# Moving the drains of VectorE and GpSimd into a hold of a matmul kernel, and giving ScalarE drains too

## The chip, the cores and the metric

The kernel runs on one core of one Trainium2 chip. The metric is the device time of the whole program in microseconds (us), as the median of several executions. A second kernel is called faster or slower when it differs by over 2%.

A *drain* is an instruction that waits until its engine has finished what it was given. Here drains are used only as filler: an engine that passes a few more instructions reaches sooner the point at which its next block of instructions is fetched from memory.

## The reference

```python
x_flat = x.reshape(-1, in_dim)            # 32768 x 256, float32
y = x_flat @ W                            # W: 256 x 256
lora_out = x_flat @ lora_A                # rank 16
lora_out = lora_out * lora_E
lora_out = lora_out @ lora_B
y = y + scale * lora_out
```

So 33.5 MB of x are read and 33.5 MB of y are written. The kernel folds the low-rank part into W once and then does one matrix product.

## The kernel before

x is cut into four chunks of 64 rows in each of 128 partitions, which live in three buffers ("homes"), so chunk 3 takes the place of chunk 0. SyncE issues all large loads (L) and stores (S) in this order:

```python
ORDER = [("A",),
    ("L", 0, 0, 16), ("L", 0, 16, 40), ("L", 0, 40, 64),
    ("L", 1, 0, 32), ("L", 1, 32, 64),
    ("L", 2, 0, 64),
    ("S", 0, 0, 40), ("S", 0, 40, 64),
    ("L", 3, 0, 32), ("L", 3, 32, 64),
    ("S", 1, 0, 64), ("S", 2, 2, 62), ("S", 3, 0, 64)]
SHARED, END_ROWS = 2, 2
SHARES = (slice(108, 113), slice(0, 108), slice(113, P))   # by GpSimd: chunk 2's first and last 2 rows
HELD = (2, 0)                       # chunk 2's first group waits ...
HOLDERS = (("S", 0, 0, 40),)        # ... for chunk 0's first store to land
VECTOR_DRAINS = 9
GPSIMD_DRAINS = 7
```

The hold divides the work of the compute engines into two bursts, one until about 54 us and one from 76 to 124 us. The rows are worked in 64 groups of four. GpSimd casts a group to bf16, TensorE transposes it, VectorE copies the transposed group out of PSUM, TensorE multiplies it, and ScalarE copies the result home.

```python
# GpSimd, after it has made the identity
for _ in range(GPSIMD_DRAINS):
    gpsimd.drain()
for g in range(N_GROUPS):
    ...                                        # waits for the group's load
    if (c, b) == HELD:
        for op in HOLDERS:
            gpsimd.wait_ge(stored[op], 16)     # the hold
    ...
    gpsimd.tensor_copy(out=stage[g % NS][:], in_=home(c)[:, b:b + CG, :])...
# VectorE, for g == 0, behind the folded weights
    for _ in range(VECTOR_DRAINS):
        vector.drain()
# TensorE
for i in range(UNROLL):                        # inside a hardware loop
    turn(i + 1, i)
    multiply(i)
```

## Time and profile before

| | before |
|---|---|
| median of 3 runs | 161.36 us (161.2 to 161.93) |
| data moved | 67.43 MB, 422 GB/s in the mean |
| TensorE busy | 94.8 us, 59% of the span |
| GpSimd, ScalarE, VectorE busy | 69.1, 66.1, 45.4 us |

The view of the costliest groups of the kernel before shows why no compute engine is the bound. Columns: line, engine, operation, tiles and shapes, count, busy us, mean ns of one, idle us before it and what ended the most of that.

```profile
L193 POOL CAST stage<-home 128x1024 bf16<-128x1024 f32 x64 | 66.3, 1042 | 50.3 <-DMA out_dram<-home 23.4
L212 ACT COPY home<-psum_y 128x1024 f32<-128x1024 f32 x64 | 64.8, 1012 | 56.1 <-PE psum_y L260 56.1
```

The busiest two helpers each idle for over 50 us. GpSimd's longest wait, 23.4 us, is for a store to land: that is the hold.

### The profile page before, as it was taken

How to read it: one execution, taken by the hardware profiler on the slowest of the kernel's cores; microseconds unless marked ns; L12 is line 12 of the kernel's file. 1: busy time of each engine (PE TensorE's matmuls, PEld its weight loads, DVE VectorE, ACT ScalarE, POOL GpSimd, SP SyncE). 2: the span in 40 equal slices, each digit the busy share in tenths (PEclk: the TensorE clock that was granted, in tenths of full speed). 3: DMA queues.
4: the chain of work that ended last, by engine and by line, in shares of the span. 5: the costliest groups of instructions: out<-in, count | busy, mean ns of one | idle time of the engine just before them, and what ended most of it. 6: DMA issues, size and time to landing. Idle time of an engine off the chain costs nothing.

```text
span 160.0 us, 2041 instructions
## 1 busy us (share of the span) xinstructions
PE 94.8 (59%) x782; PEld 83.4 (52%) x782; DVE 45.4 (28%) x66; ACT 66.1 (41%) x65; POOL 69.1 (43%) x73
## 2 busy tenths in 40 slices
PE   2769999979999600000799999999997000000000
PEld 1248999969999500000689999999996000000000
DVE  0133555545555300000135555555552000000000
ACT  3003777757777700000047777777777000000000
POOL 1074877487777000000647777777775000000000
PEclk9986999999999985555569999999999855555555
DMA  7999999999969997989999999999989996989976
GB/s 270 427 461 424 436 416 467 451 393 418 615 279 524 477 311 318 430 389 432 424 483 401 418 475 418 516 395 393 524 355 399 481 504 291 526 381 459 506 308 262
DMA packets 2451, 67.43 MB, mean 422 GB/s; under 512 B 512, under 2 KB 528, under 8 KB 784
## 3 DMA queue, kind: packets, MB, share of 16 engines
q1 hardware_dynamic: 2016, 66.60, 97.4%
q0 software_dynamic: 224, 0.52, 0.9%
q10 hardware_dynamic: 208, 0.28, 0.7%
q14 instruction: 3, 0.02, 0.0%
HBM read 33.85 MB, written 33.55 MB: 421 GB/s over the span
## 4 chain that ended last, share of the span: by engine, by line
PE 39%; DMA 35%; POOL 1%; ACT 1%; DVE 0%; issue 0%; SPq 0%; ACTq 0%; POOLq 0%; DVEq 0%
DMA out_dram<-home 30%; PE psum_y L260 25%; PE psum_xt L249 13%; DMA home<-in_x_dram 5%; POOL stage L193 1%; ACT home L212 1%; PE psum_y L282 1%; DVE weff L235 0%; SPq L146 0%; ACTq L216 0%; POOLq L192 0%; DVEq L234 0%
## 5 line engine op out<-in xcount | busy, mean ns | idle before, releaser
L193 POOL CAST stage<-home 128x1024 bf16<-128x1024 f32 x64 | 66.3, 1042 | 50.3 <-DMA out_dram<-home 23.4
L212 ACT COPY home<-psum_y 128x1024 f32<-128x1024 f32 x64 | 64.8, 1012 | 56.1 <-PE psum_y L260 56.1
L260 PE MATMUL psum_y<-weff,xt 128*128 128x256 bf16 x512 | 69.0, 280 | 0.0
L231 DVE COPY xt<-psum_xt 128x1024 bf16<-128x1024 bf16 x64 | 44.3, 692 | 68.6 <-PE psum_xt L249 68.6
L249 PE MATMUL psum_xt<-ident,stage 128*128 128x128 f32 x260 | 41.3, 283 | 25.5 <-POOL stage L193 25.3
L260 PEld LDWEIGHTS psum_y<-weff,xt 128*128 128x128 bf16 x512 | 51.5, 101 | 6.1
L249 PEld LDWEIGHTS psum_xt<-ident,stage 128*128 128x128 f32 x260 | 31.8, 146 | 28.0 <-issue 26.6
L273 PE MATMUL psum_y<-ident 128*128 128x512 f32 x4 | 3.8, 1101 | 2.9 <-POOL ident L172 2.9
L273 PEld LDWEIGHTS psum_y<-ident 128*128 128x128 f32 x4 | 1.2, 326 | 3.9 <-POOL ident L172 2.9
L221 DVE TENSOR_SCALAR ate<-psum_y,e_sb 16x256 f32<-16x256 f32 x1 | 0.5, 472 | 7.2 <-PE psum_y L276 7.2
L167 POOL DMA_DIRECT2D out_dram<-home x3 | 2.0, 676 | 1.0 <-PE psum_xt L249 1.0
L212 ACT ACT_TABLE_LOAD x1 | 1.3, 1283 | 2.1 <-SPq L295 2.1
L282 PE MATMUL psum_y<-b_sb,ate 16*128 16x256 f32 x4 | 1.1, 400 | 0.0
L170 POOL MEMSET ident<- 128x128 f32 x1 | 0.2, 205 | 1.7 <-SPq L295 1.7
L276 PEld LDWEIGHTS psum_y<-ident,a_sb 128*16 128x16 f32 x2 | 0.3, 138 | 1.2 <-issue 1.2
L235 DVE TENSOR_TENSOR weff<-w_sb,psum_y 128x512 bf16<-128x512 f32 x1 | 0.7, 686 | 0.4 <-PE psum_y L282 0.4
L282 PEld LDWEIGHTS psum_y<-b_sb,ate 16*128 16x128 f32 x4 | 0.7, 184 | 0.2 <-issue 0.2
L276 PE MATMUL psum_y<-ident,a_sb 128*16 128x128 f32 x2 | 0.6, 421 | 0.0
L172 POOL TENSOR_SCALAR_AFFINE_SELECT ident<-ident 128x128 f32<-128x128 f32 x1 | 0.3, 284 | 0.2 <-POOL ident L170 0.2
L317 POOL MEMSET const-float32-0.0<- 128x1 f32 x1 | 0.1, 93 | 0.2 <-issue 0.2
L317 POOL MEMSET const-bfloat16-1.0<- 128x1 bf16 x1 | 0.1, 97 | 0.0
L317 POOL MEMSET const-uint8-127<- 128x1 uint8 x1 | 0.1, 97 | 0.0
(1 smaller groups left out, 0.1 us busy)
## 6 DMA issues: line engine op xcount, KB each, us to landing
home<-in_x_dram SPq DMA_DIRECT2D x4, 4096.0 KB, 24.6
out_dram<-home SPq DMA_DIRECT2D x1, 7680.0 KB, 37.0
home<-in_x_dram SPq DMA_DIRECT2D x2, 3072.0 KB, 16.7
out_dram<-home SPq DMA_DIRECT2D x1, 5120.0 KB, 48.4
out_dram<-home SPq DMA_DIRECT2D x1, 3072.0 KB, 46.7
home<-in_x_dram SPq DMA_DIRECT2D x1, 2048.0 KB, 7.6
out_dram<-home POOLq DMA_DIRECT2D x1, 432.0 KB, 31.1
w_sb<-in_W_dram ACTq DMA_DIRECT2D x1, 256.0 KB, 2.7
```

The source lines that it names most:

```text
L167: engine.dma_start(out=ends_of(y_chunks[SHARED]), in_=ends_of(home(SHARED))).then_inc(landed, 16)
L193: gpsimd.tensor_copy(out=stage[g % NS][:], in_=home(c)[:, b:b + CG, :]).then_inc(s_stage[g % UNROLL], 1)
L212: scalar.copy(out=home(c)[:, b:b + CG, :], in_=psum_y[g % NY][:]).then_inc(s_free[(g + NY) % UNROLL], 1)
L221: vector.tensor_scalar(out=ate[:], in0=psum_y[0][:R, :KT, :P], scalar1=e_sb[:], scalar2=float(scale), op0=ALU.mult, op1=ALU.mult,).then_in ...
L231: vector.tensor_copy(out=xt[g % NX][:], in_=psum_xt[g % NT][:].bitcast(BF16)).then_inc(s_xt[g % UNROLL], 1)
L235: vector.tensor_add(out=weff[:], in0=w_sb[:], in1=psum_y[1][:, :KT, :]).then_inc(s_free[0], 1)
L249: ins = tensor.transpose(psum_xt[i % NT][:, b, :], words[:, b, :], ident[:])
L260: ins = tensor.matmul(psum_y[i % NY][:, b, :], xt[i % NX][:, b, t::KT], weff[:, t, :], start=(t == 0), stop=(t == KT - 1),)
L273: tensor.matmul(psum_y[1][:, :2, :], ident[:], ident[:, None, :].to_broadcast([P, 4, P]), start=True, stop=True)
L276: ins = tensor.transpose(psum_y[0][:R, t, :P], a_sb[:, t, :], ident[:])
L282: ins = tensor.matmul(psum_y[1][:, t, :], ate[:, t, :], b_sb[:], start=True, stop=True)
L317: nc = _bacc.Bacc("TRN2", target_bir_lowering=False, num_devices=1)
```

## The change

The intent: the three blocks of instructions that VectorE, ScalarE and GpSimd fetch during the run should be fetched inside the hold, once chunk 2 has landed, and at no other time. The early drains go; 12, 10 and 22 drains stand in front of group 32 instead, behind a wait for chunk 2's load.

```diff
-VECTOR_DRAINS = 9
-GPSIMD_DRAINS = 7
+VECTOR_DRAINS = 12
+GPSIMD_DRAINS = 10
+SCALAR_DRAINS = 22
...
+    def drain(engine, n):
+        for op, landed in loaded.items():
+            if op[1:3] == HELD:
+                engine.wait_ge(landed, 16)
+        for _ in range(n):
+            engine.drain()
...  gpsimd_program
-        for _ in range(GPSIMD_DRAINS):
-            gpsimd.drain()
...
             if (c, b) == HELD:
+                drain(gpsimd, GPSIMD_DRAINS)
                 for op in HOLDERS:
...  scalar_program
             c, b = g // GPC, g % GPC * CG
+            if (c, b) == HELD:
+                drain(scalar, SCALAR_DRAINS)
             scalar.wait_ge(s_y, g + 1)
...  vector_program
         for g in range(N_GROUPS):
+            if (g // GPC, g % GPC * CG) == HELD:
+                drain(vector, VECTOR_DRAINS)
             vector.wait_ge(s_turned, g + 1)
...
-                for _ in range(VECTOR_DRAINS):
-                    vector.drain()
```

## The prediction

> **What bounds the kernel now.** I read the page's slices first, then the DMA queues, then the windows by stage.
>
> ```profile
> DMA  7999999999969997989999999999989996989976
> GB/s 270 427 461 424 436 416 467 451 393 418 615 279 524 477 311 318 430 389 432 424 483 401 418 475 418 516 395 393 524 355 399 481 504 291 526 381 459 506 308 262
> q1 hardware_dynamic: 2016, 66.60, 97.4%
> q14 instruction: 3, 0.02, 0.0%
> HBM read 33.85 MB, written 33.55 MB: 421 GB/s over the span
> ```
>
> The DMA row stays at 9 from the second slice to the last few (a lone 6 or 7 is a large packet counted in the slice in which it starts). The queue of the big loads and stores takes 97.4% of what 16 DMA engines have in the span. So this is a copy of 67 MB with arithmetic under it; the time changes only if a DMA engine has less to do, or waits less. The queue named instruction is the one that the change is about: three packets, nearly nothing.
>
> Then the stages (columns: stretch, its length, busy time of PE, PEld, DVE, ACT, POOL, granted clock, DMA share, GB/s):
>
> ```profile
> 8.00:58.00 50.00, 44.34 (x380) 39.69 (x380) 22.83 (x33) 31.37 (x31) 33.06 (x32) 0.97 1.00 433
> 58.00:62.00 4.00, 0.00 (x0) 0.00 (x0) 0.00 (x0) 0.00 (x0) 0.00 (x0) 0.61 1.14 354
> 62.00:75.00 13.00, 0.00 (x0) 0.00 (x0) 0.00 (x0) 0.00 (x0) 0.00 (x0) 0.50 0.97 420
> 125.00:154.00 29.00, 0.00 (x0) 0.00 (x0) 0.00 (x0) 0.00 (x0) 0.00 (x0) 0.54 0.97 419
> 154.00:160.00 6.00, 0.00 (x0) 0.00 (x0) 0.00 (x0) 0.00 (x0) 0.00 (x0) 0.50 0.70 300
> ```
>
> No compute engine works in 58 to 75 us (the hold) or after 125 us, while the DMA share is 0.97 to 1.14: the hold costs the transfers nothing. The longest pieces of the chain and the waits name what ends the hold:
>
> ```profile
> 27.18 48.41 DMA out_dram<-home
> 75.70 1.05 POOL stage L193
> ...
> POOL stage L193 <- DMA out_dram<-home: 23.4, 1, 23.4
> ```
>
> The first store of chunk 0 is issued at 27.18 and lands at 75.59, and GpSimd, 23.4 us idle, starts at 75.70. The last store is issued at 124.28, and the store before it, still moving then, lands at 140.4. So the compute has 16 us of slack before the DMA engines would run dry.
>
> Last, I cut the DMA view into stretches to place the three fetches. The stretches 55 to 56, 80 to 81 and 107 to 108 us answer in turn, and all others from 0 to 160 us show no such row:
>
> ```profile
> q14 instruction: 1, 0.01, 2.1%
> ...
> q14 instruction: 1, 0.01, 1.9%
> ...
> q14 instruction: 1, 0.01, 1.9%
> ```
>
> From here on I use the trace's packet records, which I strung into 16 back-to-back chains, one for each DMA engine, by matching each packet's start to another's end. The names of the chains (A, B, C) are mine. Fetches start at 55.72 (chain A, 333 ns), 80.22 (chain B, 309 ns) and 107.74 us (chain C, 309 ns). No chain is idle for over 0.1 us from 6 us on.
>
> **What the Trainium skill says.**
> - "Runtime: NRT & Kernel Launch", section "Instruction fetch mechanics": an engine's instructions are streamed into a small buffer, and its sequencer drives a DMA queue of its own that fetches the next block while the present one runs; blocks of 16 KiB. The trace agrees on a separate queue; its packets have 8192 bytes, half the page's block.
> - "DMA: Bandwidth & Descriptors", section "Queues, rings and completion order": a DMA engine takes turns between its queues, a packet at a time. The trace agrees: the first fetch starts at 55.719, where a 65536-byte packet of chain A ends (55.722).
> - The same page, "Why a DMA increments its semaphore by 16 and not by 1": engines finish independently, and only all 16 mean that the data is there. The trace agrees: chunk 2's load has 15 landings by 62.62 and the last at 63.49; the hold's store has 15 by 74.72 and the last at 75.59.
> - "Perfetto Trace Analysis", section "Per-engine timelines" (sequencer-only instruction): of a drain the profile reports the execution alone, not its wait. The trace has drains of 10 ns, 40 ns apart, on VectorE, and of 34 ns, 61 ns apart, on GpSimd.
>
> **The change part by part.**
>
> *Removed at the start.* VectorE's 9 drains run from 11.83 to 12.18 us, and its next copy starts at 12.28 on TensorE's transposes, which end at 12.24. GpSimd's 7 end at 3.26, and its first cast waits for data until 8.05. Neither was on the path: 0 us.
>
> *Added in the hold.* VectorE 12 x 40 ns = 0.5 us; GpSimd 10 x 61 ns = 0.6 us; ScalarE 22, about 1 us if 40 to 50 ns apart (an estimate from the other two engines). They start when chunk 2 has landed (63.49 now, near 62.6 if no engine is late) and so end near 64, about 10 us before the store lands. These engines are idle until 75.7 anyway: 0 us.
>
> *Do the fetches move?* A fetch seems to follow the count of instructions an engine has issued. At 107.74 ScalarE has issued 64; the packet ahead on chain C began at 105.33, when it had issued 62. With the change it has 40 + 22 = 62 behind it in the hold and a copy queued: just enough, so the third fetch should be ScalarE's. VectorE has 49 issued in the hold now and 52 after; GpSimd has 57 and a wait, and some 60 after; the fetch at 80.22 comes when they have 50 and 61. So the two early fetches are theirs in some order, and all three should fall at 63 to 66 us (start of the drains, plus at most the 1.5 us packet under way on each chain). I give 0.8 to all three moving.
>
> *What a fetch costs its DMA engine.* Chain C: 0.31 us plus 0.16 us by which the next packet is longer than the median of its size: 0.47 us. Chain B: 0.31 + 0.09 = 0.40 us. Chain A is worse: at the end of chunk 2's load it is at 63.15, the other fifteen at 61.6 to 62.3, mean about 61.9: 1.25 us behind. At the end of chunk 3's load it is at 102.45 against about 100.7: 1.8 us behind. A chain that arrives late at a turn from loads to stores seems to lose again there. Moved behind the landing, A's fetch should cost 0.45 us and the first such loss should go: A gains 0.8 us by 75 us and 0.8 to 1.3 us in all.
>
> *What that is worth at the end.* The shares of chunk 2 that GpSimd stores are cut so that late chains carry less: A and C get 8 KB, most others 41 KB, some 1.2 us more. The last packets end, in order from the back, at 159.60 (A), 159.49, 159.39, 159.32 (B), 159.24 and so on down to 158.50 (C). If A falls to about 158.5, the next chain, which never carried a fetch, still ends at 159.49. So the sum is 159.60 - 159.49 = 0.11 us off the end. B and C only exchange one time of fetch for another. The hold should end at about 74.9, being the last other chain's 74.7 plus what a fetched chain lags, 0.7 us earlier, but this only starts compute with slack sooner. 161.36 - 0.1, rounded with a little hope for the other turns: 161.2 us.
>
> **The rivals.**
> *1. The fetch on A feeds the slow spot.* In 58 to 62 us, just after the first fetch, all sixteen chains have one packet that takes 3.5 to 3.8 us in place of 2.42 (354 GB/s in the window above). If the late chain or its fetch causes that, 1.2 us go for all: 160.1 us. For it: the time. Against it: the other two fetches are followed by nothing like it, and the packets begin to be slow 2.4 us after the fetch. I give it 0.12.
> *2. Three chains late where one was.* The fetches now all come ahead of the hold's store landing and the turns at 82 and 100 us; if each late chain loses 0.5 us or more at each turn, and B, which carries a full share, becomes last: 159.32 + 0.5 to 1 gives 0.2 to 0.7 us more, so 161.6 to 162.1 us. Against it: B was 0.4 us late at 100 us already and lost only 0.08 us there. 0.15.
> *3. A fetch starves an engine.* The steady period of 1.31 us in the second burst goes on over the fetch at 107.74, so nothing is starved now, and nothing will be. A stall of a few us would also be swallowed by the slack of 16 us. 0 us either way.
> *4. Drains are too few*, and a fetch comes when compute resumes at 75 us: the same cost on the same chain, and the same end. 161.2 to 161.4 us.
>
> **Range and chances.** The main path gives 161.2; the three runs of before spread by 0.7 us on their own. Rival 1 reaches 160.1, rival 2 162.1, each with a small chance. I take 160.6 to 161.7. Two per cent would be 3.2 us, more than all fetches and the slow spot together: faster 0.01, within 2% 0.98, slower 0.01.
>
> **What would show it.** All three instruction packets between 62 and 67 us and none later; chunk 2's load with all 16 landings within 0.7 us; the hold's end near 74.9; chain A no longer the last, and the last packet at 159.4 to 159.6; 67.4 MB as before. Wrong would be: the slow spot at 58 to 62 us gone (rival 1), the chains of the fetches last by over 0.3 us (rival 2), or fetches still at 75 to 110 us (rival 4, and the count of drains misjudged).

## The result, and the profile after

| | before | after |
|---|---|---|
| median of 6 runs each | 161.65 us (161.03 to 162.02) | 161.35 us (161.2 to 161.38) |
| ratio | | 0.9983, 95% interval 0.9958 to 1.0008 |
| drains in the hold | none | 12 VectorE at 62.73 to 63.19 us, 10 GpSimd at 62.79 to 63.38 us |
| instruction fetches | 55.72, 80.22, 107.74 us | 67.83, 67.84, 84.82 us |
| chunk 2's load: 15th and 16th landing | 62.62, 63.49 us | 62.57, 62.70 us |
| hold's store: 15th and 16th landing | 74.72, 75.59 us | 75.02, 75.04 us |
| last landing of all | 159.94 us | 159.99 us |

A ratio is the mean time of one kernel's fast runs over that of the other's of the same rounds, so it is not quite the ratio of the medians.

The slices and the instruction queue of the page after:

```profile
DMA  7999999999969997999999999989979997989986
q14 instruction: 3, 0.02, 0.0%
```

The DMA row is as full as before, and there are still three fetches. The DMA view in the stretches 67 to 69 and 84 to 86 us of the changed kernel places them:

```profile
q14 instruction: 2, 0.02, 1.9%
...
q14 instruction: 1, 0.01, 1.0%
```

Two came into the hold, a few us later than intended; the third did not. The chain and the waits of the changed kernel show the hold's end:

```profile
29.86 45.17 DMA out_dram<-home
75.09 1.05 POOL stage L200
...
POOL stage L200 <- DMA out_dram<-home: 21.2, 1, 21.2
```

It ends at 75.09 us, 0.6 us earlier than before (75.70). (The store is issued later, at 29.86 us, because TensorE ran slowly for longer at the start of this execution: a multiplication took 421 ns in place of 272 until about 17 us, not 14. The changed kernel's second trace, after_again, has 27.18 us again. It does not reach the end of the hold.) Last, the stages, with columns as in the prediction:

```profile
58.00:62.00 4.00, 0.00 (x0) 0.00 (x0) 0.00 (x0) 0.00 (x0) 0.00 (x0) 0.67 1.15 365
62.00:75.00 13.00, 0.00 (x0) 0.00 (x0) 0.00 (x0) 0.00 (x0) 0.00 (x0) 0.50 0.97 418
125.00:154.00 29.00, 0.00 (x0) 0.00 (x0) 0.00 (x0) 0.00 (x0) 0.00 (x0) 0.50 0.97 415
```

The rates are within about 3% of those before, the slow stretch at 58 to 62 us included (365 GB/s against 354).

So 0.6 us were won at the hold and none at the end, as the DMA engines were full either way. Where did ScalarE's drains go? The timeline of the changed kernel (start, us, engine, line and operation, idle before it and its releaser):

```profile
79.11 1.01 ACT L221 COPY home<-psum_y 128x1024 f32<-128x1024 f32 x1 [21.80 <-PE psum_y L269]
...
81.45 1.93 ACT L221 COPY home<-psum_y 128x1024 f32<-128x1024 f32 x2 [1.33 <-PE psum_y L269]
...
82.52 0.14 PEld L258 LDWEIGHTS psum_xt<-ident,stage 128*128 128x128 f32 x1 [0.29 <-ACT home L221]
```

The copy at 79.11 is that of group 31. TensorE turns group 32 before it multiplies group 31, and group 32 is what the hold holds; so group 31's copy waits for the hold's end too (21.80 us), and ScalarE's drains, which stand behind it, run at 80.2 to 81.4 us, after the hold. There they delay the next copy to 81.45 and cost TensorE a wait of 0.29 us, which the slack of the compute takes up.

### The profile page after: what moved, and what is told of

Its sections match the earlier page's. It is cut to its first block, busy times and chain, and to the rows that moved or that the text cites. A ratio compares the mean times of both kernels' runs of the same rounds, so it can differ in the third digit from the quotient of the medians.

```text
span 160.0 us, 2070 instructions
## 1 busy us (share of the span) xinstructions
PE 96.5 (60%) x782; PEld 84.4 (53%) x782; DVE 45.4 (28%) x66; ACT 66.0 (41%) x65; POOL 69.3 (43%) x73
## 4 chain that ended last, share of the span: by engine, by line
PE 38%; DMA 33%; ACT 3%; POOL 1%; issue 1%; ACTq 0%; SPq 0%
DMA out_dram<-home 28%; PE psum_y L269 24%; PE psum_xt L258 13%; DMA home<-in_x_dram 5%; ACT home L221 3%; POOL stage L200 1%; PE psum_y L291 1%; SPq L147 0%; ACTq L175 0%; ACTq L225 0%
## 5 line engine op out<-in xcount | busy, mean ns | idle before, releaser
L258 PE MATMUL psum_xt<-ident,stage 128*128 128x128 f32 x260 | 42.2, 286 | 22.3 <-POOL stage L200 22.3
L258 PEld LDWEIGHTS psum_xt<-ident,stage 128*128 128x128 f32 x260 | 32.4, 148 | 25.2 <-issue 23.6
L291 PE MATMUL psum_y<-b_sb,ate 16*128 16x256 f32 x4 | 2.1, 670 | 0.0
L291 PEld LDWEIGHTS psum_y<-b_sb,ate 16*128 16x128 f32 x4 | 1.2, 320 | 0.5 <-issue 0.3
```

The source lines that it names most:

```text
L258: ins = tensor.transpose(psum_xt[i % NT][:, b, :], words[:, b, :], ident[:])
L291: ins = tensor.matmul(psum_y[1][:, t, :], ate[:, t, :], b_sb[:], start=True, stop=True)
```

## The experiments

Three jobs of four kernels, five rounds each, every job on another chip. A kernel under test has 6 runs; the old kernel ran 11 times beside each job. "Chains" are the DMA engines as strung together from the packet records. For these experiments I rebuilt them with one more condition, that an engine moves exactly 8 packets of each large transfer: the one-line matching of the prediction had confused some of them.

### The changed kernel again (after_again, after_third), and the old one as a candidate (before_again)

No edit in any of the three.

> The changed kernel unaltered, for its spread. Theory T1 (a fetch ahead of the turn from chunk 2's load to the first store makes one DMA engine late by 1.2 us or more, and how late depends on where it falls, so the old kernel's times spread): this one stays within 161.2 to 161.5 us, while the runs of the kernel before beside it spread over 161.0 to 162.0. Rival T2 (the spread of before is chance of the chip that day): both spread by about the same. Its trace: two fetches at 66 to 70 us, the third, ScalarE's, behind the hold at about 85 us.

Measured: 161.24 us (161.03 to 161.48), ratio 0.9977; the old kernel beside it 161.56 (161.07 to 162.06). Fetches at 68.08, 68.09 and 84.98 us.

> The kernel before, unaltered, for its spread and one more trace. Theory T1: over 1 us from the fastest to the slowest run, and if the traced execution is one of 161.8 us or more, its trace has a DMA engine that is later at the turns than in the trace at hand (over 1.2 us behind the others at chunk 2's landing, or a last packet over 160.0 us). Rival: a slow execution shows no late engine, and all sixteen are later by the same.

Measured: 161.25 us (161.16 to 161.44), ratio 0.9986 *to itself*: the old kernel beside it had 161.61 (161.08 to 161.92). Its traced execution was not slow, so no slow one was seen in a trace.

> The changed kernel a third time, in another place of the order: 161.2 to 161.4 us if its level is its own; 161.0 us if the lead of the kernel without drains was the order's. Level with the old kernel when that ran as one of the four (161.25 us).

Measured: 161.10 us (160.96 to 161.36), ratio 0.9985. Between the two expectations, 0.1 us from each.

What follows: the spread of the old kernel's runs, which I had put down to its first fetch, is absent when the same code runs in the place of a candidate. T1 fails there. The 0.3 us between the medians of the first result need no effect of the change: the old program compared with itself gives 0.9986 (interval 0.9967 to 1.0005), the changed one 0.9983, 0.9977 and 0.9985, all inside that interval. In like places, though in different jobs, the old kernel has 161.25 us and the changed one 161.35, 161.24 and 161.10. The change moves the time by nothing that can be told from zero. Why the old kernel's runs beside a job spread by 1 us is left open.

The second trace of the old kernel also tests what the prediction rests on. Its first fetch is at 56.04 us, but chunk 2's load has its last two landings only 0.35 us apart (0.87 in the first trace). The engine with that fetch ends at 158.89 us, 0.67 us ahead of the last one, which carries no fetch and ends at 159.56. So chain A's large lag and its last place belong to one execution of the old kernel and not to the kernel.

### No drains at all (none, none_again)

```diff
-VECTOR_DRAINS = 12
-GPSIMD_DRAINS = 10
-SCALAR_DRAINS = 22
+VECTOR_DRAINS = 0
+GPSIMD_DRAINS = 0
+SCALAR_DRAINS = 0
```

> No drains anywhere. By the counts of issued instructions at which the fetches were asked for so far (VectorE about 43, ScalarE about 55, GpSimd about 59 of the traced ones), all three fetches fall in the second burst: VectorE's and GpSimd's at 83 to 95 us, ScalarE's near 107 us. T1: nothing is fetched ahead of the turn at 58 to 62 us, so no engine is late there, and the time is that of the changed kernel, 161.2 to 161.5 us, with a small spread: the drains of before did the harm, and those of after only undo it. Rival T3 (the hold is a better place for a fetch than a burst): slower than the changed kernel by 0.3 us or more, 161.7 us.

Measured: 161.00 us (160.87 to 161.02), ratio 0.9963. The fetches came at 79.27, 88.44 and 105.19 us, all behind the hold. T1 had forecast 161.2 to 161.5 us, so it misses here too.

> The kernel without drains once more, now behind another program and beside the changed kernel. If the 0.2 us by which it led the kernels with drains belongs to it: 160.9 to 161.1 us again, and 0.15 us or more under the changed kernel of the same job. If it was the chip's or the order's: within 0.1 us of that one.

Measured: 161.02 us (160.90 to 161.30), ratio 0.9981; beside it the changed kernel (after_third) had 161.10. So the lead is 0.24 us in the first job and 0.08 us in the third: the level fits the first expectation, the lead the second, and whether there is a lead stays undecided. The wait for the hold's store in the first of these (none):

```profile
POOL stage L200 <- DMA out_dram<-home: 22.2, 1, 22.2
```

The hold there ends at 74.64 us, earlier than in any kernel with a fetch between chunk 2's last packets and the store's landing (75.09 to 75.99 us). The store's 15th and 16th landings are at 74.33 and 74.43 us. The next run, which has drains but no fetch so early, agrees with 74.45 us. The hold was not a better place for the fetches (T3 falls).

### The drains behind all work (drains_at_end)

```diff
-            if (c, b) == HELD:
-                drain(scalar, SCALAR_DRAINS)
...
+        drain(scalar, SCALAR_DRAINS)      # and likewise for the two others, behind their last work
```

> All 44 drains are in the program, but behind each engine's last work, where they bring no fetch forward; the code has the changed kernel's length. If the gain of the run without drains (161.0 us) comes from where its fetches fall, this is 160.9 to 161.1 us as well, with fetches at about 79, 88 and 105 us. If that gain was chance, or the code's length, it is 161.2 to 161.4 us like the changed kernel.

Measured: 161.02 us (160.96 to 161.34), ratio 0.9977, fetches at 89.35, 100.28 and 105.04 us: all behind the hold, though two later than expected. The code is as long as the changed kernel's and the time is that of the kernel without drains. So if there is a lead, it does not go with the length of the code. No changed kernel ran in this job: beside it the old one as a candidate had 161.25 us.

### ScalarE's drains really in the hold (act_in_hold)

```diff
-            if (c, b) == HELD:
+            if ((g + 1) // GPC, (g + 1) % GPC * CG) == HELD:
                 drain(scalar, SCALAR_DRAINS)
```

> ScalarE's 22 drains one group earlier, ahead of the copy of group 31, which itself waits for the hold's end; so they run at chunk 2's landing, near 63 us, and its fetch comes at 66 to 70 us with the two others in place of about 85 us. T1: a fetch is a fetch once it is behind the turn, so 161.2 to 161.5 us as the changed kernel. T3: 0.2 us faster than the changed kernel, 161.1 us.

Measured: 161.18 us (161.10 to 161.46), ratio 0.9976. The DMA view from 67 to 69 us, then the timeline:

```profile
q14 instruction: 3, 0.02, 2.9%
...
81.77 1.01 ACT L221 COPY home<-psum_y 128x1024 f32<-128x1024 f32 x1 [1.20 <-PE psum_y L269]
```

One group earlier, ScalarE's drains start at 62.71 us and its fetch joins the two others, at 68.03, 68.11 and 68.11 us. This shows that group 31's copy was what kept them out of the hold. The second line is the next copy: it now starts when TensorE's product is done (81.73 us), with no drains in between. The time is that of the changed kernel, so the miss cost nothing.

### Drains at the start of the hold (no_landing_wait)

```diff
     def drain(engine, n):
-        for op, landed in loaded.items():
-            if op[1:3] == HELD:
-                engine.wait_ge(landed, 16)
         for _ in range(n):
...  (GpSimd's drains moved ahead of its wait for the load)
```

> VectorE's and GpSimd's drains as in the changed kernel, but without the wait for chunk 2's landing: they run at the start of the hold, 53 to 56 us, and with some three packets of 2.4 us ahead of each fetch these come at about 60 to 63 us, at the turn from load to store. T1: two engines are late by 1 us or more at the end of chunk 2's load, the hold ends at 75.4 us or later, and the time is 0.3 to 0.7 us over that of the changed kernel: 161.6 to 162.0 us. Rival T2 (places of fetches do not matter): 161.2 to 161.5 us.

Measured: 161.17 us (161.14 to 161.22), ratio 0.9976. Only one fetch moved to the turn, at 62.08 us; the others came at 80.22 and 86.18. By the count of issued instructions the one at 80.22 should be GpSimd's, whose drains stop at 61 issued: one or a few too few. The engine hit is late, though not quite as expected: its last packet of the load ends on time, at 62.09 us, and the fetch comes between it and the word of its landing. Chunk 2's load has 15 landings by 62.64 and the last at 63.44, and the waits read

```profile
POOL stage L198 <- DMA out_dram<-home: 22.9, 1, 22.9
```

with the hold's end at 75.42 us. But the time is not 0.3 us over the changed kernel, it is level. An engine that is late at the turn costs the hold 0.8 us (74.64 without drains, in the same job) and the end nothing that can be seen.

### One more fetch for two engines (double_fetch)

```diff
-VECTOR_DRAINS = 12
-GPSIMD_DRAINS = 10
+VECTOR_DRAINS = 144
+GPSIMD_DRAINS = 142
```

> The changed kernel with 132 more drains on each of VectorE and GpSimd behind chunk 2's landing, so that each fetches one more block[...] within the hold: the cost of a fetch by itself. VectorE 144 x 40 ns = 5.8 us and GpSimd 142 x 61 ns = 8.7 us still end by 72 us. If a fetch costs its DMA engine 0.66 to 0.69 us, as the two at 67.8 us of the changed kernel did, and nothing takes it off again: two engines 0.6 us later at the hold's store, the hold's end at 75.6 us or later, and the time 0.4 to 0.7 us over the changed kernel, 161.7 to 162.0 us, since the last of those two ends level with the last of the others already. If the fetches are hidden: 161.2 to 161.4 us.

Measured: 161.76 us (161.70 to 161.90), ratio 1.0022; beside it the changed kernel had 161.10. The page and, below it, the DMA view from 72 to 77 us:

```profile
q14 instruction: 5, 0.04, 0.1%
...
q14 instruction: 2, 0.02, 0.8%
```

Two fetches more, at 73.15 and 76.16 us, the second behind the hold's end (75.99). The kernel is 0.66 us slower than the changed one beside it, clear of the noise. The hold's store has its last landing at 75.94 us. It is that of the engine with the fetches at 67.96 and 73.15 us: the two cost it 1.46 us within the store, each being 0.31 to 0.32 us and a next packet 0.36 and 0.48 us longer.

But the 0.66 us are not shown to be the price of these fetches. In the trace that engine ends at 159.71 us, and the one that ends last, at 160.07, carries no fetch. Its packets of the hold's store take up to 1.68 us in place of 1.51, 0.55 us in all, from 63.4 to 73.0 us, just while the added drains run (62.6 to 71.8 us); in the changed kernel they all take 1.51. So the 264 drains may cost something by themselves, and no run separates the two. What a single fetch costs is seen on its engine alone, and the time did not show it in any other run. Where had those fetches their slack?

### Equal shares (none_equal_shares)

```diff
-SHARES = (slice(108, 113), slice(0, 108), slice(113, P))
+SHARES = (slice(0, P),)
```

> Without drains, and GpSimd's shares of chunk 2 as one transfer of 128 partitions, 8 for each DMA engine, in place of 10 or 11 for twelve engines and 2 for four. If the four lightened engines are those that carry the three fetches and the one with longer packets in chunk 1's store, these now end last: 6 more packets of 159 ns or so, about 1.0 us, against a loss on the others of 0.3 us: 161.6 to 162.0 us. If the shares did not matter, 161.0 us.

Measured: 161.75 us (161.72 to 162.05), ratio 1.0018: 0.75 us over the kernel without drains. In the traces of before and after, the chain with the fetch at 55.72 us, those at 80.22 and 107.74, and a fourth without a fetch have 2 packets of GpSimd's shares, the twelve others 8 to 12. With equal shares each has 8. Then that fourth chain ends last, at 160.22 us, the three with fetches end at 159.14 to 159.34, and the rest earlier. So the uneven shares take the fetches in: each light chain is spared about 8 packets of 159 ns, 1.3 us, an estimate from those packets. But the 0.75 us are the fourth chain's, whose 64 KB packets take about 0.15 us more each in chunk 1's store. The three with fetches end only 0.14 to 0.34 us behind the last of the others (159.00), so without the fourth equal shares would have cost about that (an estimate from these ends). The fourth is also the engine that ends last in double_fetch.

### Chunk 2's load in halves (none_split_l2), and the first store between them (none_store_early)

```diff
-    ("L", 2, 0, 64),
-    ("S", 0, 0, 40),
+    ("L", 2, 0, 32),
+    ("L", 2, 32, 64),      # none_split_l2: the store follows here
+    ("S", 0, 0, 40),       # none_store_early: the store between the halves
```

> Without drains, and chunk 2's load in two halves, so that its packets have 32 KB in place of 64 KB. All 16 engines have one packet about 1.2 us too long at the end of this load, in every trace so far, and none at the end of chunk 3's load, whose packets have 32 KB. If the size of the last packet makes it, the loss goes and the time is 160.0 us, faster than all so far. If the turn from pure load to pure store with no compute running makes it, or something at 58 us of the clock, it stays: 161.0 us, with the long packets again at 58 to 62 us.

Measured: 161.08 us (160.97 to 161.29), ratio 0.9974. The loss stays and is now spread over the last two packets of 32 KB of each engine, 0.7 and 0.5 us.

> Without drains; chunk 2's load in two halves with the first store of chunk 0 between them. All traces so far have all 16 engines slow at 58 to 62 us, the end of chunk 2's load, 1.0 to 1.3 us each in the mean, and hardly any loss at the end of chunk 3's load, when the compute engines run. If the loss belongs to a turn from load to store that no compute accompanies, the turn now at 52 us, in the first burst, is free, the later ones may lose, and the time is 160.0 to 160.8 us. If it belongs to this store following a load, the loss comes at 49 to 52 us; if to 58 to 62 us of the clock, it stays there; in both 161.0 us.

Measured: 161.42 us (161.13 to 163.30), ratio 1.0026: no gain. But the loss moved. The view by stages of none and of none_store_early, 57 to 63 us:

```profile
57.00:63.00 6.00, 0.00 (x0) 0.00 (x0) 0.00 (x0) 0.00 (x0) 0.00 (x0) 0.63 0.83 284
```

```profile
57.00:63.00 6.00, 0.00 (x0) 0.00 (x0) 0.00 (x0) 0.00 (x0) 0.00 (x0) 0.76 1.01 437
```

The stretch runs at full rate, and by the packet records the sixteen engines lose 0.95 us each in the mean at 48 to 52 us instead, where the first half of the load now ends, while all compute engines are busy. So the loss has nothing to do with the fetches, the hold or the clock time: it goes with the program's first large store following a load. What makes it is open. At the end of chunk 3's load, which stores follow too, it is nearly absent.

## Why the prediction was right or wrong

The time was right: 161.2 us forecast, 161.35 measured, within 160.6 to 161.7. Its class, "same", was right. Neither says much for the steps, since the old kernel's 161.65 and 161.25 us lie in that range as well. By its steps:

- **The bound.** Right. The DMA rows of before and after are alike, and five kernels with the fetches at other places between 62 and 108 us (none, none_again, drains_at_end, act_in_hold, no_landing_wait) lie at 161.00 to 161.18 us.
- **Removed drains and added drains cost nothing.** Right for VectorE and GpSimd (0.5 and 0.6 us at 62.7 to 63.4). ScalarE's cost TensorE 0.29 us behind the hold, inside the slack.
- **"All three should fall at 63 to 66 us".** Wrong in two ways. The step that failed for ScalarE was "40 + 22 = 62 behind it in the hold and a copy queued": the copy of group 31 comes ahead of the drains and waits for the hold's end, so the fetch came at 84.82 us; act_in_hold shows it. For the two others "at most the 1.5 us packet under way" was wrong: they came at 67.8, some 4.5 us behind the last drains, about three packets of 1.51 us. At 84.82 us, with packets of 1.21 us, the delay behind the start of the last drain (81.27) was 3.55 us, again about three.
- **What a fetch costs.** Mis-sized where it falls among the hold's stores: 0.66 to 0.70 us there, in place of 0.45. The extra loss of a late engine at the turn was there in this trace (landings 0.87 us apart before, 0.13 after), and the hold's end came at 75.09, with 74.9 forecast. But it was taken from one execution: in before_again the landings are 0.35 us apart. The reading of the slow spot was also short, as chain A's own packet there took 4.03 us, above the 3.5 to 3.8 given for all.
- **The end: "159.60 - 159.49 = 0.11 us off".** Not seen: the last chain ended at 159.67 and carried a fetch again. The step that failed was "If A falls to about 158.5". The fetches moved, but two chains now pay 0.7 us each. That alone does not put them last: at 138.9 us, after the light shares, both are level with the others (138.4 to 139.1). They fall behind in the last store, where five 64 KB packets of each take 2.45 to 2.61 us in place of 2.42 and one packet of GpSimd's shares takes 0.67 and 0.81 us in place of 0.16. Why is open. And the start of the sum, chain A as the last one, does not hold in before_again. Also "B, which carries a full share" was an error of my chain matching: all three chains with fetches are light.
- **Rivals.** 1 fell: 365 GB/s in the slow stretch with the fetch gone from before it, 354 with it, and the stretch follows the store, not the fetch. 2 fell in its time: three chains fetching at 68 us (act_in_hold) gave 161.18 us. 3 held: no gap of a few us. 4 happened for ScalarE, by another cause, and cost nothing, as it said.
- **Never in the prediction:** that the old kernel compared with itself gives 0.9986. What looked like a small gain is of that size.

The lowest times are those of the kernel with no drains, 161.00 and 161.02 us. Its lead over the changed kernel is 0.08 to 0.24 us, about 0.1%, and not settled; that it would come from the fetches lying behind the hold is argued and not shown.

## What to carry to other kernels

Where the transfers are the bound, moving a small cost between places helps only if it comes off the DMA engine that ends last; look at the engines' single ends and shares before moving it, and in more than one trace, since another engine can be the last in the next execution. Before an instruction is put "in a hold", ask of each engine separately what it is waiting on there: an engine a stage further down may still have the previous group ahead of it. And for effects of a few parts in a thousand, run the old kernel as a candidate too.

## What the Trainium skill lacked or had wrong

- "Runtime: NRT & Kernel Launch", section "Instruction fetch mechanics", gives blocks of 16 KiB (256 instructions); every fetch in these traces has 8192 bytes, and 132 more instructions of 64 bytes on an engine brought one more (double_fetch).
- The same section calls the cost "mostly hidden". For the engines that run the instructions nothing here contradicts it: none has a gap of a few us at a fetch. It does not tell what a fetch costs a DMA engine that is full: 0.31 us for the packet and mostly 0.1 to 0.5 us on the next one.
- "DMA: Bandwidth & Descriptors", section "Queues, rings and completion order", has an engine take turns between its queues packet by packet. The fetches do start at a packet's end, but about three packets behind the last of the drains that brought them on (4.5 us with packets of 1.51 us, 3.55 us with 1.21 us); no page tells of that delay.
- No page has the loss of about 1 us on all sixteen DMA engines where the first large store follows a load (1.03 us in the mean in none, 0.95 us in none_store_early, moved with the store).
